# A hybrid decoder layer in which the first phase is put into program order and two query projections move between the attention's first blocks

## The chip, the cores and the metric

The kernel runs on one core of one Trainium2 chip. The metric is the device time of one execution in microseconds. Before the change it is 905.42 us (median of three runs, 904.74 to 907.59).

## The reference, cut to what matters

```python
h = rmsnorm(x, norm_mix_g)                       # 512 tokens x 1024
proj = h @ w_in                                  # one wide projection, split by columns
qk_ml, v_ml, o_ml, if_pre, q_sw, k_sw, v_sw, g_a, g_b = split(proj)
qk_ml = silu(causal_depthwise_conv(qk_ml, conv)) # 4 heads of q and k for the mLSTM
h_ml  = mlstm_chunkwise(q_ml, k_ml, v_ml, ig, lf)
y_a   = sigmoid(o_ml) * rmsnorm(h_ml)
y_b   = swa_with_sinks(q_sw, k_sw, v_sw, sinks)  # window 128, 16 query heads, 4 key heads of 64
merged = sigmoid(g_a) * (y_a @ w_branch_a) + sigmoid(g_b) * (y_b @ w_branch_b)
x = x + merged @ w_out
x = x + square(relu(rmsnorm(x) @ w_up)) @ w_down
x = x + sigmoid(rmsnorm(x) @ w_ple_gate) * (p @ w_ple_proj)
return rmsnorm(x, final_norm_g)
```

## The kernel before, in words

Tokens are handled in four tiles of 128. All large products are made from float32 operands cut into a high and a low part: ScalarE rounds the high part into `wh` (or `h`, `qs`, `yb`), VectorE subtracts it from the original and leaves the low part (`split`, lines 139 and 140). A product of two such numbers is three TensorE products, high by high, low by high, high by low (`pairs`), so one tile of 128 outputs over 1024 inputs is 24 products (`mm_T`, `mm_tok`, `chain`, line 168). A weight comes by a load from SyncE's queue into one of four `wr` buffers, and its parts go into one of four `wh` and four `wl` buffers (`load_w`).

The first phase is lines 202 to 314. A gain row is loaded into the first row of a cleared tile `grow`, and two TensorE products with a tile of ones spread it over all partitions into PSUM (`gmix`, line 251). `stir` (line 246) issues products of ones by ones that nobody reads, nine ahead of `gmix` and four behind it. `norm(m)` squares a tile of x on ScalarE (268), takes the root there (258) and the reciprocal on VectorE (260), and scales the tile in two halves (272). `turn(m)` transposes it in two groups of four blocks (285) and splits the result into `h`; `values(m)` multiplies it by 264 columns of weights in three pieces (`vsif`: attention values and mLSTM gates) and stores `vs` (297) and `gt` (299). A scheduler decides in which order each engine takes these instructions. Behind them come the two key projections (`proj_T` with `w_ksw`), the gate scans, the output gates, the mLSTM values and two gate projections.

The sliding-window attention starts with query projections 0 and 1. It then runs over 16 units of 128 queries (`units`), four heads each. `swa_probs` makes a unit's scores (636) from two query projections, reduces them on VectorE with their maximum (644), takes exponentials on ScalarE (655) and normalises (659). `swa_turn` transposes the result (670) and ScalarE copies it out (672); `swa_out` multiplies two units with the values (683). Scores and transposes take turns in two PSUM buffers, tag `a`. Units 0 to 3 use queries 0 and 1, units 4 to 7 queries 2 and 3, units 8 to 15 the other four. The remaining projections are a stock of single products, `pieces`, from which each step of the loop takes 18 to fill TensorE (708). In this stretch TensorE's order is written out by hand (`manual_schedule`); that of ScalarE and VectorE is the scheduler's.

After the loop the eighth q/k projection (`qk_proj(7)`) is made, then `silu` on all eight, the mLSTM weights (`ml_weights`, 770 to 778) and, between them, the products of branch b (`branch_b`).

Of the kernel before, what the change touches and what calls it, by code (L numbers as in the profile page):

```python
# [10 lines left out]
F32 = mybir.dt.float32  # L11
# [26 lines left out]
def block_kernel(  # L38
# [73 lines left out]
    def act_hl(n="s"):  # L112
        return [act_r(n), act_r(n)]
# [9 lines left out]
    def tok_scratch(n="lm"):  # L123
        return sp.tile([P, LMW], F32, tag="lm", bufs=LMB, name=nm(n))[:, :D]
# [5 lines left out]
    def small(n, w, bufs=4):  # L130
        return cp.tile([P, w], F32, tag=f"{n}{w}", bufs=bufs, name=nm(n))
# [4 lines left out]
    def split(dst, src, scale=None):  # L136

        if scale is None:
            done = A.copy(dst[0], src)  # L139
            V.tensor_sub(dst[1], src, r32(dst[0]))  # L140
# [48 lines left out]
    def mm_tok(ps, w, acts, m, first=True, last=True):  # L189

        ops = []
        for k in range(len(acts)):
            ops += pairs([q[:, m * P : (m + 1) * P] for q in acts[k]], [q[:, k, :] for q in w])
        chain(ps, ops, first, last)

    nc.scalar.preload_act_table_set("sqrt_and_others")


    ident = cp.tile([P, P], F32, name="ident")
    make_identity(nc, ident)  # L200
    ones = cp.tile([P, P], F32, name="ones")
    V.memset(ones, 1.0)
    eps_t = cp.tile([P, 1], F32, name="eps_t")
    V.memset(eps_t, EPS)
    zeros4 = c1.tile([4, P], F32, name="zeros4")
# [25 lines left out]
    V.memset(grow, 0.0)  # L231
    nc.sync.dma_start(out=grow[:1, :], in_=g_mix)
# [9 lines left out]
    idle = ps_a()  # L242

    def stir(n):
        for i in range(n):
            tc.keep_in_program_order(T.matmul(idle[:, :P], ones, ones, start=True, stop=True))

    stir(9)
    gmix = ps_a()
    for c in range(2):  # L250
        T.matmul(gmix[:, c * 512 : (c + 1) * 512], ones, grow[:, c * 512 : (c + 1) * 512], start=True, stop=True)
    stir(4)

    def rstd_of(ss, n):

        w = ss.shape[1]
        sd = small("sd", w)
        A.activation(sd, ss, AF.Sqrt, bias=eps_t, scale=1.0 / n)
        rs = small("rs", w, 5)
        V.reciprocal(rs, sd)  # L260
        return rs

    xns = []

    def norm(m):
        xn = tok_scratch("xn")
        ss = small("ss", 1)
        A.activation(xn, xt[m], AF.Square, accum_out=ss)
        rs = rstd_of(ss, D)
        for c in range(2):  # L270
            o = slice(c * 512, (c + 1) * 512)
            V.scalar_tensor_tensor(xn[:, o], xt[m][:, o], rs, gmix[:, o], ALU.mult, ALU.mult)
        xns.append(xn)

    vs = []
    gt = c1.tile([P, NT, 8], F32, name="gt")
    h2, hT = big_hl("h")
    hf = []

    def turn(m):  # L280
        wide = ps_a() if m == NT - 1 else None
        for kq in range(2):
            ps = wide[:, kq * 512 : (kq + 1) * 512] if wide is not None else ps_t()
            for k in range(4):
                T.transpose(ps[:, k * P : (k + 1) * P], xns[m][:, kq * 512 + k * P : kq * 512 + (k + 1) * P], ident)
            done = split(
                [t[:, 4 * kq : 4 * kq + 4, m * P : (m + 1) * P] for t in h2],
                ps.rearrange("p (k c) -> p k c", k=4),
            )
        return done  # L290

    def values(m):
        ps = ps_g()
        for (k0, n), w in zip(vsif, wv):
            mm_tok(ps[:, :264], w, hT[k0 : k0 + n], m, first=k0 == 0, last=k0 == 6)
# [25 lines left out]


    HALF = [slice(0, 64), slice(64, 128)]
    keys = []
    for i in range(2):
        ps = proj_T(w_ksw, i, ps_t)
        keys.append(act_hl("kk"))
        split(keys[i], ps)


    gml = cols(g_ml, KT, "gml", c1)
# [259 lines left out]
    def q_proj(i):  # L591
        ps = proj_T(w_qsw, i)
        q_done(i, ps)
# [11 lines left out]
    def qk_proj(i):  # L605
        qk_done(i, proj_T(w_qkml, i))
# [21 lines left out]
    def swa_probs(kp, gp, n):  # L628
        k0 = max(n - 1, 0) * P
        ls = ps_a()  # L630
        for g in range(2):
            q = qs[kp * 4 + 2 * gp + g]
            for i, (x, y) in enumerate(((0, 0), (0, 1), (1, 0))):
                for ab in range(2):
                    o = ls[:, ab * 512 + g * 256 : ab * 512 + (g + 1) * 256]
                    T.matmul(  # L636
                        o, q[x][HALF[ab], n * P : (n + 1) * P], keys[kp][y][HALF[ab], k0 : k0 + 256], start=i == 0, stop=i == 2
                    )
        W = P if n == 0 else 2 * P
        sk = sinks_of[:, kp, :, gp, :]  # L640
        lm3 = tok_scratch().rearrange("p (g k) -> p g k", g=4)[:, :, :W]
        mx = small("mx", 4)
        for g in range(4):
            V.tensor_tensor_reduce(  # L644
                lm3[:, g, :], ls[:, g * 256 : g * 256 + W], band[:, 256 - W :], 0.125, sk[:, g // 2, g % 2 : g % 2 + 1], ALU.add, ALU.max, mx[:, g : g + 1]
            )
# [12 lines left out]
        V.tensor_tensor(lm3, lm3, rc.unsqueeze(2).broadcast_to([P, 4, W]), ALU.mult)  # L659
        probs[kp, gp, n] = lm3  # L660
# [37 lines left out]

    def pieces():

        order = [("q", 3), ("k", 0), ("q", 4), ("q", 5), ("k", 4), ("q", 6), ("q", 7), ("k", 1), ("k", 5), ("k", 2), ("k", 6), ("k", 3)]
        for kind, i in order:
            w = load_w((w_qsw if kind == "q" else w_qkml)[i], KT * P, KT)
            ps = ps_g()
            for k in range(KT):
                ops = pairs([t[:, k, :] for t in w], hT[k])
                for j, (l, r) in enumerate(ops):
                    T.matmul(ps, l, r, start=k == 0 and j == 0, stop=k == KT - 1 and j == 2)  # L708
                    yield
            (q_done if kind == "q" else qk_done)(i, ps)  # L710

    fill = pieces()
    with tc.manual_schedule(engines={mybir.EngineType.PE}):
# [535 lines left out]
```

## Time and profile before

| what | value |
|---|---|
| median of three runs | 905.42 us |
| the profiled execution, whole | 905.38 us |
| its span, first to last instruction | 903.5 us |
| mean granted TensorE clock | 0.999 |
| bytes moved | 100.50 MB, mean 111 GB/s |

The profile is of one execution. Its rows name an engine, a line of the kernel, an operation and the tiles written and read; an idle time stands in brackets with the instruction that ended it. TensorE is called PE and its weight loads PEld, VectorE DVE, ScalarE ACT, GpSimd POOL, and SyncE's queue SPq. The time outside the span, 905.38 - 903.5 = 1.9 us, belongs to no instruction.

### The profile page before, as it was taken

The numbers are of one execution on the slowest core, as the hardware profiler recorded it, in microseconds if no ns is written. First come the engines' busy times: TensorE is split into PE (matmuls) and PEld (weight loads), VectorE is DVE, ScalarE is ACT, GpSimd is POOL, SyncE is SP. The second block draws the span as 40 slices with busy tenths as digits, with TensorE's granted clock in tenths as the row PEclk, the third lists the DMA queues.
The fourth block names the chain that finished last, engine by engine and source line by source line (L and its number), as shares of the span: only waits on it lengthen the run. The fifth ranks groups of instructions, "written<-read, shape, count | busy, mean of one in ns | idle before, by whom it ended". The sixth has DMA issues, their size and how long they took to land.

```text
span 903.5 us, 12111 instructions
## 1 busy us (share of the span) xinstructions
PE 886.6 (98%) x4676; PEld 741.2 (82%) x4676; DVE 645.9 (71%) x1030; ACT 451.4 (50%) x757; POOL 23.7 (3%) x40
## 2 busy tenths in 40 slices
PE   8999999999899999999999999999999999999996
PEld 7888899997677777878888888888888888888886
DVE  6884687874777787567644578757966885798466
ACT  6373444444666568675322545334434443444843
POOL 0011000000000000000310000000000000000000
PEclk9999999999999999999999999999999999999999
DMA  7543134435121133234552620631262044102302
GB/s 249 198 155 124 47 109 155 158 118 163 48 68 51 47 106 118 81 96 161 162 194 87 218 86 0 209 118 47 68 211 94 1 164 155 55 24 72 139 1 94
DMA packets 29965, 100.50 MB, mean 111 GB/s; under 512 B 4173, under 2 KB 4685, under 8 KB 29906
## 3 DMA queue, kind: packets, MB, share of 16 engines
q1 hardware_dynamic: 27938, 93.15, 30.9%
q0 software_dynamic: 1824, 6.30, 2.0%
q8 instruction: 37, 0.61, 0.3%
q10 hardware_dynamic: 144, 0.26, 0.1%
q14 instruction: 22, 0.18, 0.1%
HBM read 91.30 MB, written 8.40 MB: 110 GB/s over the span
## 4 chain that ended last, share of the span: by engine, by line
PE 72%; DVE 2%; ACT 1%; DMA 0%; issue 0%; SPq 0%; DVEq 0%; ACTq 0%
PE psg L168 35%; PE psp L168 22%; PE psg L708 7%; PE pst L168 2%; PE psa L670 2%; PE psa L636 1%; PE pst L683 1%; PE pst L777 1%; PE psp L882 1%; DVE wl L140 0%; DMA ptok<-in_p 0%; PE pst L829 0%; DVE uf L140 0%; ACT lm L655 0%; DVE lm L644 0%
## 5 line engine op out<-in xcount | busy, mean ns | idle before, releaser
L139 ACT CAST wh<-wr 128x1024 fp32r<-128x1024 f32 (+1 forms) x137 | 142.9, 1045 | 208.6 <-PE psg L168 62.8
L140 DVE TENSOR_TENSOR wl<-wr,wh 128x1024 fp32r<-128x1024 f32 (+1 forms) x137 | 171.1, 1253 | 100.4 <-ACT wh L139 91.4
L168 PE MATMUL psg<-x,wh 128*128 128x512 f32 x512 | 158.4, 390 | 0.0
L168 PE MATMUL psp<-wh,uf 128*128 128x512 f32 x448 | 139.1, 390 | 0.0
L168 PEld LDWEIGHTS psg<-x,wh 128*128 128x128 f32 x512 | 96.0, 188 | 19.9
L168 PE MATMUL psg<-x,wl 128*128 128x512 f32 x256 | 99.7, 389 | 0.0
L168 PEld LDWEIGHTS psp<-wh,uf 128*128 128x128 f32 x448 | 84.1, 188 | 17.3
L168 PE MATMUL psp<-wl,uf 128*128 128x512 f32 x224 | 87.2, 389 | 0.0
L139 ACT CAST wh<-wd 128x1024 fp32r<-128x1024 f32 x44 | 46.3, 1054 | 57.9 <-PE psp L168 26.1
L708 PE MATMUL psg<-h,wh 128*128 128x512 f32 x192 | 60.7, 397 | 0.0
L140 DVE TENSOR_TENSOR wl<-wd,wh 128x1024 fp32r<-128x1024 f32 x44 | 53.4, 1218 | 4.4 <-ACT wh L139 4.1
L168 PEld LDWEIGHTS psg<-x,wl 128*128 128x128 f32 x256 | 48.1, 188 | 9.8
L168 PE MATMUL psa<-h,wh 128*128 128x256 f32 (+1 forms) x256 | 55.1, 311 | 0.0
L168 PEld LDWEIGHTS psp<-wl,uf 128*128 128x128 f32 x224 | 42.1, 188 | 8.7
L140 DVE TENSOR_TENSOR uf<-F,uf 128x1792 fp32r<-128x1792 f32 (+2 forms) x20 | 33.0, 1650 | 21.8 <-ACT uf L139 21.8
L168 PEld LDWEIGHTS psa<-h,wh 128*128 128x128 f32 x256 | 41.9, 191 | 3.5 <-ACT p L557 0.7
L168 PE MATMUL psg<-yb,wh 128*128 128x512 f32 x128 | 42.7, 406 | 0.3 <-DVE gb L817 0.2
L139 ACT CAST uf<-F 128x1792 fp32r<-128x1792 f32 (+2 forms) x20 | 27.9, 1397 | 26.4 <-DVE F L958 26.2
L168 PE MATMUL psg<-ya,wh 128*128 128x512 f32 x128 | 40.6, 395 | 0.0
L944 DVE SCALAR_TENSOR_TENSOR rt<-psg,rB 128x512 f32<-128x512 f32 x32 | 22.0, 688 | 25.6 <-PE psg L168 25.6
L708 PEld LDWEIGHTS psg<-h,wh 128*128 128x128 f32 x192 | 34.9, 188 | 6.6
L168 PE MATMUL psg<-h,wh 128*128 128x512 f32 x128 | 40.2, 394 | 0.0
(284 smaller groups left out, 1742.0 us busy)
## 6 DMA issues: line engine op xcount, KB each, us to landing
wr<-in_w_up SPq DMA_DIRECT2D x32, 512.0 KB, 3.4
wd<-in_w_down SPq DMA_DIRECT2D x24, 512.0 KB, 4.5
wr<-in_w_o SPq DMA_DIRECT2D x8, 512.0 KB, 4.3
gd<-gr POOLq DMA_DIRECT2D x8, 512.0 KB, 3.0
wr<-in_w_qsw SPq DMA_DIRECT2D x8, 512.0 KB, 4.2
wr<-in_w_qkml SPq DMA_DIRECT2D x8, 512.0 KB, 3.2
wr<-in_w_b SPq DMA_DIRECT2D x8, 512.0 KB, 3.3
gl<-gd SPq DMA_DIRECT2D x8, 512.0 KB, 3.2
```

What stands on the lines that cost most here:

```text
L139: done = A.copy(dst[0], src)
L140: V.tensor_sub(dst[1], src, r32(dst[0]))
L168: last_mm[0] = T.matmul(ps, l, r, start=first and i == 0, stop=last and i == len(ops) - 1, skip_group_check=parts)
L636: T.matmul(o, q[x][HALF[ab], n * P : (n + 1) * P], keys[kp][y][HALF[ab], k0 : k0 + 256], start=i == 0, stop=i == 2)
L670: T.transpose(pt[:, c : c + P], lm3[:, g, j * P : (j + 1) * P], ident)
L683: T.matmul(o[HALF[ab], m * 256 : (m + 1) * 256], vs[n + m + 1 - nk + j][:, c : c + 64], pTs[m][:, j * 512 + ab * 256 : j * 512 + (ab + 1) ...
L708: T.matmul(ps, l, r, start=k == 0 and j == 0, stop=k == KT - 1 and j == 2)
L777: T.matmul(psc[:, n0:], qk[4 + h][:, n0 : n0 + P], qk[h][:, n0:], start=True, stop=True)
L882: T.transpose(ps[:, m * P : (m + 1) * P], xk[m][:, k * P : (k + 1) * P], ident)
L944: V.scalar_tensor_tensor(a, ps, 0.0, rB, ALU.max, ALU.mult)
```

## The change

The change has two parts that don't touch each other.

In the first phase, PE, ACT and DVE now take their instructions in the order in which the code is written (`manual_schedule` over all three). `ones` and half of `grow` are cleared by GpSimd, the load of the gain row stands right behind the first tile of x, and the two halves of `gmix` have a PSUM tile each. The work of `norm`, `turn` and `values` is cut into smaller helpers, and the products of the first tile follow the order in which their operands are made: the high parts with the first weights, then the low weights, then the low activations. The same products are made as before.

In the attention, queries 2 and 3 are projected whole ahead of unit 0's and unit 1's scores, 16 products of the stock follow, and each step of the loop takes 17. The eighth q/k projection joins the stock, which is 12 projections, 288 products, as before: 16 + 16 x 17.

```diff
+    ones = cp.tile([P, P], F32, name="ones")
+    G.memset(ones, 1.0)
+    grow = tok_scratch("grow")
+    G.memset(grow[:, :512], 0.0)
+    V.memset(grow[:, 512:], 0.0)
     ident = cp.tile([P, P], F32, name="ident")
     make_identity(nc, ident)
-    ones = cp.tile([P, P], F32, name="ones")
-    V.memset(ones, 1.0)
...
-    grow = tok_scratch("grow")
-    V.memset(grow, 0.0)
+    load_x(0, 2)
     nc.sync.dma_start(out=grow[:1, :], in_=g_mix)
-    load_x(0, 2)
...
-    gmix = ps_a()
+    gmix = [ps_a()[:, :512] for _ in range(2)]
     for c in range(2):
-        T.matmul(gmix[:, c * 512 : (c + 1) * 512], ones, grow[:, c * 512 : (c + 1) * 512], start=True, stop=True)
+        T.matmul(gmix[c], ones, grow[:, c * 512 : (c + 1) * 512], start=True, stop=True)
     stir(4)
...
-    norm(0)
-    turn(0)
-    wv = [load_w(None, n * 264, n, raw) for (_, n), raw in zip(vsif, wv)]
-    norm(1)
-    values(0)
-    norm(2)
-    turned = turn(1)
-    with tc.issue_after(turned):
-        norm(3)
-    values(1)
-    turn(2)
-    turn(3)
-    values(2)
-    gate_in = values(3)
+    early, late, every = range(4), range(4, 8), range(8)
+    plain = [("hi", early), ("lo w", early), ("lo h", early), ("hi", late), ("lo w", late), ("lo h", late)]
+    with tc.manual_schedule(engines={mybir.EngineType.PE, mybir.EngineType.Activation, mybir.EngineType.DVE}):
+        norm(0)
+        w_high(0)
+        scaled(0)
+        w_low(0)
+        t_ = [turn(0, kq) for kq in range(2)]
+        high(0, 0, t_[0])
+        low(0, 0, t_[0])
+        w_high(1)
+        high(0, 1, t_[1])
+        w_low(1)
+        low(0, 1, t_[1])
+        w_high(2)
+        w_low(2)
+        norm(1)
+        scaled(1)
+        ps0 = products(0, [("hi", early), ("lo w", range(3)), ("lo h", early), ("hi", late), ("lo w", range(3, 8)), ("lo h", late)])
+        t_ = [turn(1, kq) for kq in range(2)]
+        norm(2)
...
+        scaled(2)
+        ps1 = products(1, plain)
+        norm(3)
+        values(0, ps0)
+        scaled(3)
...
+        values(1, ps1)
+        ps2 = products(2, plain)
+        ps3 = products(3, plain)
+        values(2, ps2)
+        gate_in = values(3, ps3)
...
-        order = [("q", 3), ("k", 0), ("q", 4), ("q", 5), ("k", 4), ("q", 6), ("q", 7), ("k", 1), ("k", 5), ("k", 2), ("k", 6), ("k", 3)]
+        order = [("k", 0), ("q", 4), ("q", 5), ("k", 4), ("q", 6), ("q", 7), ("k", 1), ("k", 5), ("k", 2), ("k", 6), ("k", 3), ("k", 7)]
...
     with tc.manual_schedule(engines={mybir.EngineType.PE}):
+        q_proj(2)
         swa_probs(*units[0])
-        q_proj(2)
+        q_proj(3)
         swa_probs(*units[1])
+        more(16)
         for u in range(16):
             if u + LOOK < 16:
                 swa_probs(*units[u + LOOK])
             pT = swa_turn(*units[u])
-            for _ in range(18):
-                next(fill)
+            more(17)
...
-    qk_proj(7)
```

The new helpers split the old ones: `high` and `low` are the two lines of `split` for one group of four blocks, `w_high` and `w_low` those for a piece of the 264 columns, `products` issues a tile's 24 products in a given order, and `more(n)` takes n products from the stock.

How this moves instructions is seen at three places. The first is ACT at the start. In the rows, `xn` is the scaled tile, `ss` its sum of squares, `sd` the root, `wh` a weight's high part and `h` the transposed tile's. Before:

```order
L268 ACTIVATE xn_141,ss_142<-xt_101 128x1024 [waits DMAHW1_49,DMAHW0_49]
L258 ACTIVATE sd_144<-ss_142,eps_t 128x1 [waits DVE_49,Activation_49]
L139 CAST wh_164<-wr_110 128x792 [waits DMAHW2_49]
L139 CAST wh_168<-wr_112 128x792 [waits DMAHW4_49]
L139 CAST wh_172<-wr_114 128x528 [waits DMAHW5_49]
L139 CAST h_139<-pst_150 128x4x128 [waits PE_49]
L268 ACTIVATE xn_176,ss_177<-xt_102 128x1024 [waits DMAHW6_49]
L139 CAST h_139<-pst_157 128x4x128 [waits PE_49]
```

and after the change:

```order
L273 ACTIVATE xn_143,ss_155<-xt_104 128x1024 [waits DMAHW1_49,DMAHW0_49]
L275 ACTIVATE sd_157<-ss_155,eps_t 128x1 [waits DVE_49,Activation_49]
L305 CAST wh_147<-wr_111 128x792 [waits DMAHW3_49]
L295 CAST h_141<-pst_165 128x4x128 [waits PE_49]
L305 CAST wh_148<-wr_113 128x792 [waits DMAHW4_49]
L295 CAST h_141<-pst_170 128x4x128 [waits PE_49]
L305 CAST wh_149<-wr_115 128x528 [waits DMAHW5_49]
L273 ACTIVATE xn_144,ss_183<-xt_105 128x1024 [waits DMAHW6_49]
```

The second and third weight piece have moved behind the first tile's transposed halves, and the square of the second tile behind both.

The second place is DVE at the start: `rs` is the reciprocal root, `psa` the spread gain in PSUM, `wl` a weight's low part, and `h` now the transposed tile's low part. Before:

```order
L260 RECIPROCAL rs_146<-sd_144 128x1 [waits Activation_49]
L140 TENSOR_TENSOR wl_165<-wr_110,wh_164 128x792 [waits DMAHW2_49,Activation_49]
L272 SCALAR_TENSOR_TENSOR xn_141<-xt_101,rs_146,psa_131 128x512 [waits DMAHW0_49,DVE_49,PE_49]
L272 SCALAR_TENSOR_TENSOR xn_141<-xt_101,rs_146,psa_131 128x512 [waits DMAHW1_49]
L140 TENSOR_TENSOR wl_169<-wr_112,wh_168 128x792 [waits DMAHW4_49,Activation_49]
L140 TENSOR_TENSOR h_140<-pst_150,h_139 128x4x128 [waits Activation_49]
```

and after the change:

```order
L277 RECIPROCAL rs_159<-sd_157 128x1 [waits Activation_49]
L282 SCALAR_TENSOR_TENSOR xn_143<-xt_104,rs_159,psa_132 128x512 [waits DMAHW0_49,DVE_49,PE_49]
L282 SCALAR_TENSOR_TENSOR xn_143<-xt_104,rs_159,psa_133 128x512 [waits DMAHW1_49,PE_49]
L308 TENSOR_TENSOR wl_150<-wr_111,wh_147 128x792 [waits DMAHW3_49,Activation_49]
L299 TENSOR_TENSOR h_142<-pst_165,h_141 128x4x128 [waits Activation_49]
L308 TENSOR_TENSOR wl_151<-wr_113,wh_148 128x792 [waits DMAHW4_49,Activation_49]
```

Both scaled halves have moved ahead of the first weight, and each now waits for PE by itself, since each reads a PSUM tile of its own.

The third place is PE where the attention starts: the first row of each run of products, with `psg` the bank of a query projection (later of the stock), `psa` a unit's scores from keys `kk` and queries `qs`, or a transposed unit from `lm`; the products left out between them are the rest of each run. Before:

```order
L168 MATMUL psg_2079<-h_139,wh_2082 128x512
L636 MATMUL psa_2116<-kk_387,qs_2075 128x256 x2
L168 MATMUL psg_2150<-h_139,wh_2153 128x512
L636 MATMUL psa_2185<-kk_387,qs_2075 128x256 x2
L636 MATMUL psa_2219<-kk_387,qs_2075 128x256 x2
L670 MATMUL psa_2253<-ident,lm_2129 128x128 x4
```

and after the change:

```order
L168 MATMUL psg_2122<-h_141,wh_2125 128x512
L697 MATMUL psa_2157<-kk_393,qs_2081 128x256 x2
L168 MATMUL psg_2191<-h_141,wh_2194 128x512
L697 MATMUL psa_2226<-kk_393,qs_2081 128x256 x2
L769 MATMUL psg_2266<-h_141,wh_2262 128x512
L697 MATMUL psa_2283<-kk_393,qs_2081 128x256 x2
L731 MATMUL psa_2317<-ident,lm_2170 128x128 x4
```

Query 2 (psg_2150 before, psg_2122 now) stands ahead of unit 0's scores, query 3 ahead of unit 1's, and the first 16 products of the stock (psg_2266) between unit 1's and unit 2's.

More of the change, by code (lines that the diff above doesn't have):

```diff
@@ L240, in block_kernel @@
     nc.sync.dma_start(out=bif, in_=b_if.broadcast_to([P, 8]))
-    idle = ps_a()
+    idle = ps_g()
     def stir(n):
@@ L261, in rstd_of @@
         return rs
[L263 to L273, printed above, removed]
     vs = []
@@ L278, in block_kernel @@
     hf = []
[L280 to L290, printed above, removed]
@@ L292, in values, with norm @@
-    def values(m):
-        ps = ps_g()
-        for (k0, n), w in zip(vsif, wv):
-            mm_tok(ps[:, :264], w, hT[k0 : k0 + n], m, first=k0 == 0, last=k0 == 6)
+    xns = [tok_scratch("xn") for _ in range(NT)]
+    rss = {}
+    def norm(m):
+        ss = small("ss", 1)
+        A.activation(xns[m], xt[m], AF.Square, accum_out=ss)
+        sd = small("sd", 1)
+        A.activation(sd, ss, AF.Sqrt, bias=eps_t, scale=1.0 / D)
+        rss[m] = small("rs", 1, 5)
+        V.reciprocal(rss[m], sd)
@@ new lines, in scaled, with turn, parts @@
+    def scaled(m):
+        for c in range(2):
+            o = slice(c * 512, (c + 1) * 512)
+            V.scalar_tensor_tensor(xns[m][:, o], xt[m][:, o], rss[m], gmix[c], ALU.mult, ALU.mult)
+    def turn(m, kq):
+        ps = ps_t()
+        for k in range(4):
+            T.transpose(ps[:, k * P : (k + 1) * P], xns[m][:, kq * 512 + k * P : kq * 512 + (k + 1) * P], ident)
+        return ps
+    def parts(m, kq):
+        o = slice(4 * kq, 4 * kq + 4)
+        return [t[:, o, m * P : (m + 1) * P] for t in h2]
@@ new lines, in high, with low, w_high @@
+    def high(m, kq, ps):
+        return A.copy(parts(m, kq)[0], ps.rearrange("p (k c) -> p k c", k=4)).ins
+    def low(m, kq, ps):
+        hi, lo = parts(m, kq)
+        return V.tensor_sub(lo, ps.rearrange("p (k c) -> p k c", k=4), r32(hi)).ins
+    wvh = [wp.tile([P, 1024], F32R, tag="wh", bufs=WB, name=nm("wh"))[:, : n * 264] for _, n in vsif]
+    wvl = [wp.tile([P, 1024], F32R, tag="wl", bufs=WB, name=nm("wl"))[:, : n * 264] for _, n in vsif]
+    def w_high(i):
+        A.copy(wvh[i], wv[i][:, : vsif[i][1] * 264])
@@ new lines, in w_low, with products @@
+    def w_low(i):
+        V.tensor_sub(wvl[i], wv[i][:, : vsif[i][1] * 264], r32(wvh[i]))
+    def products(m, order):
+        ps = ps_g()
+        where = {k0 + k: (i, k) for i, (k0, n) in enumerate(vsif) for k in range(n)}
+        done = 0
+        for kind, ks in order:
+            for k in ks:
+                i, c = where[k]
+                act = hT[k][1 if kind == "lo h" else 0][:, m * P : (m + 1) * P]
+                w = (wvl if kind == "lo w" else wvh)[i][:, c * 264 : (c + 1) * 264]
+                last_mm[0] = T.matmul(ps[:, :264], act, w, start=done == 0, stop=done == 3 * KT - 1)
+                done += 1
+        return ps
@@ L296, in values @@
+    def values(m, ps):
         t = sp.tile([P, 256], F32, tag="vs", bufs=4, name=nm("vs"))
@@ L299, in values @@
         return V.tensor_add(gt[:, m, :], ps[:, 256:264], bif)
-    norm(0)
-    turn(0)
-    wv = [load_w(None, n * 264, n, raw) for (_, n), raw in zip(vsif, wv)]
-    norm(1)
-    values(0)
-    norm(2)
-    turned = turn(1)
-    with tc.issue_after(turned):
-        norm(3)
-    values(1)
-    turn(2)
-    turn(3)
-    values(2)
-    gate_in = values(3)
+    early, late, every = range(4), range(4, 8), range(8)
[19 more added lines that the diff above has]
+        norm(2)
+        high(1, 0, t_[0])
+        high(1, 1, t_[1])
+        low(1, 0, t_[0])
+        low(1, 1, t_[1])
+        scaled(2)
+        ps1 = products(1, plain)
+        norm(3)
+        values(0, ps0)
+        scaled(3)
+        t_ = [turn(2, kq) for kq in range(2)]
+        q = [ps_a()[:, :512] for _ in range(2)]
+        for kq in range(2):
+            high(2, kq, t_[kq])
+            low(2, kq, t_[kq])
+        for kq in range(2):
+            for k in range(4):
+                T.transpose(q[kq][:, k * P : (k + 1) * P], xns[3][:, kq * 512 + k * P : kq * 512 + (k + 1) * P], ident)
+        for kq in range(2):
+            turned = [high(3, kq, q[kq]), low(3, kq, q[kq])]
+        values(1, ps1)
[3 more added lines that the diff above has]
+        gate_in = values(3, ps3)
+    turned.append(last_mm[0].ins)
     def proj_T(wd, i, bank=ps_g):
@@ L323, in block_kernel @@
     HALF = [slice(0, 64), slice(64, 128)]
[L324 to L328, printed above, removed]
+    with tc.issue_after(turned[0]), tc.issue_after(turned[1]), tc.issue_after(turned[2]):
+        keys = []
+        for i in range(2):
+            ps = proj_T(w_ksw, i, ps_t)
+            keys.append(act_hl("kk"))
+            split(keys[i], ps)
     gml = cols(g_ml, KT, "gml", c1)
@@ L712, in block_kernel, with more @@
     fill = pieces()
+    def more(n):
+        for _ in range(n):
+            next(fill)
     with tc.manual_schedule(engines={mybir.EngineType.PE}):
+        q_proj(2)
         swa_probs(*units[0])
-        q_proj(2)
+        q_proj(3)
         swa_probs(*units[1])
+        more(16)
         for u in range(16):
```

## The prediction

> **What bounds the kernel now.** I read the page first, then the table of stretches, then TensorE's waits, then the timeline of the places where TensorE waits.
>
> ```profile
> PE 886.6 (98%) x4676; PEld 741.2 (82%) x4676; DVE 645.9 (71%) x1030; ACT 451.4 (50%) x757; POOL 23.7 (3%) x40
> ```
>
> TensorE (PE) is busy for 98% of the span, so the other engines matter only where PE waits for them. The next view shows where that is. A row gives start:end, its length, then the busy time of PE, of its weight loads (PEld), of VectorE (DVE), ScalarE (ACT) and GpSimd.
>
> ```profile
> 0.00:32.00 32.00, 28.79 (x172) 24.56 (x173) 19.92 (x36) 18.53 (x32) 2.05 (x11) 1.00 0.75 264
> 30.50:200.00 169.50, 169.49 (x1048) 151.44 (x1047) 128.14 (x158) 78.61 (x96) 8.54 (x19) 1.00 0.36 124
> 220.00:230.70 10.70, 7.79 (x55) 6.37 (x53) 6.46 (x28) 3.33 (x12) 0.00 (x0) 1.00 0.28 100
> 230.70:243.60 12.90, 12.56 (x80) 9.55 (x78) 9.84 (x30) 9.64 (x32) 0.00 (x0) 1.00 0.13 41
> 243.60:336.20 92.60, 92.59 (x587) 71.80 (x587) 71.34 (x211) 60.34 (x165) 0.00 (x0) 1.00 0.18 58
> 336.20:362.00 25.80, 25.29 (x109) 19.55 (x108) 21.13 (x37) 20.31 (x44) 0.00 (x0) 1.00 0.41 142
> ```
>
> From 30.5 to 200 us PE is never idle, and in most of the attention (243.6 to 336.2) neither. What can be won lies in the first 30 us and around 216 to 244 us. PE's waits there, in total, times, longest:
>
> ```profile
> PE psa L670 <- DVE mx L644: 2.9, 1, 2.9
> PE psa L636 <- DVE qs L140: 1.2, 2, 0.9
> PE psa L636 <- ACT qs L139: 0.9, 1, 0.9
> PE pst L777 <- DVE dm L778: 0.5, 1, 0.5
> ```
>
> The first three are 5.0 us, all at the attention's start.
>
> **The change, term A: until the first tile is turned.** These are rows of the timeline: start, length, engine, line, operation, and in brackets the idle time before.
>
> ```profile
> 1.06 4.21 PE L246 MATMUL psa<-ones 128*128 128x128 f32 x18 [1.06 <-DVE eps_t L204]
> 1.30 0.91 DVE L231 MEMSET grow<- 128x1024 f32 x1 [0.16 <-issue]
> 1.66 0.42 SPq L149 DMA_DIRECT2D wr<-in_w_vsif  x1
> 2.24 0.30 SPq L232 DMA_DIRECT2D grow<-in_g_mix  x1
> 5.99 3.75 PE L251 MATMUL psa<-grow,ones 128*128 128x512 f32 x4 [0.73 <-DMA grow<-in_g_mix]
> 6.03 0.16 DVE L260 RECIPROCAL rs<-sd 128x1 f32<-128x1 f32 x1 [3.82 <-ACT sd L258]
> 9.54 1.26 PE L246 MATMUL psa<-ones 128*128 128x128 f32 x8
> 9.78 1.41 DVE L272 SCALAR_TENSOR_TENSOR xn<-xt,rs,psa 128x512 f32<-128x512 f32 x2 [1.50 <-PE psa L251]
> 10.68 1.22 PE L285 MATMUL pst<-ident,xn 128*128 128x128 f32 x8
> 28.83 0.62 PE L168 MATMUL pst<-h,wh 128*128 128x512 f32 x2
> ```
>
> The gain row is loaded at 2.24, because DVE clears 1024 columns of its tile until 2.21; a weight load has gone ahead of it at 1.66. PE idles 0.73 us for it. After the change GpSimd and DVE clear 512 columns each, and the load stands ahead of the weights. Half of 0.91 us puts its issue at 1.66, so it lands some 0.6 us earlier or more; PE then goes on at 5.27, where its first row ends: **0.7 us**.
>
> Next come the two broadcasts of the gain, four records in 3.75 us, and four filling matmuls, eight records in 1.26 us. Eighteen records of the same filling matmuls took 4.21 us before 5.27, so PE ran at half its rate until about 9.54. When it doubles in the changed kernel the trace can't show. It can be no earlier than 5.27, since 4.21 us of unbroken work didn't bring it; as recorded it came 3.55 us after the gap. Between those ends I take the middle, 7.4. Then the broadcasts are issued at 5.27 and 6.98, the second speeds up after a quarter, and PE is through at 8.04; the fillers take 0.85 more, and the first tile's transposes start at 8.9 instead of 10.68. DVE doesn't hold them: its first half waits for the first broadcast only (7.2), and takes 0.74. **Term A: -1.8 us.** If PE keeps the half rate until 9.54, the transposes start at 9.97 (-0.7); if it doubles at 5.27, at 7.85 (-2.8).
>
> The Trainium skill (TensorE: Matmul & The Clock Gate, Part 1: The HAM clock gate) says that the array runs at half rate until it has been busy through one window of about 3.4 us, that the windows run freely, and that the doubling thus comes 3.4 to 6.8 us after work begins. For work unbroken from 1.06 us that is 4.5 to 7.9 us. By this rule, which the row at 9.54 fits if the 0.73 us gap spoilt a window, term A would lie between -1.6 and -2.8; the rule speaks against the half rate until 9.54.
>
> **Term B: from the first transposes to the first key projection.** Before, this took 28.83 - 10.68 = 18.15 us.
>
> ```profile
> 8.60 0.63 ACT L139 CAST wh<-wr 128x528 fp32r<-128x528 f32 x1 [0.32 <-DMA wr<-in_w_vsif]
> 15.56 1.03 PE L285 MATMUL pst<-ident,xn 128*128 128x128 f32 x8
> 16.19 1.07 ACT L139 CAST h<-pst 128x512 fp32r<-128x512 f32 x2
> 17.15 1.07 ACT L268 ACTIVATE xn<-xt 128x1024 f32<-128x1024 f32 x1
> 25.83 0.40 PE L168 MATMUL psg<-wh,h 128*128 128x264 f32 x2
> 28.71 0.28 PE L168 MATMUL psg<-wh,h 128*128 128x264 f32 x1
> ```
>
> Products of one tile: from 25.83 to 28.71, 24 at 0.12 = 2.88 us. Eight transposes take about 0.9. Four tiles are 15.1 us at best, so 3.0 us were waits.
>
> The first tile gets worse. ACT now rounds weight pieces 1 and 2 behind the first tile's halves (before, both were done by 9.23), and squares tile 1 after that. From the first transposes: 0.6 until four are out, then ACT 0.5 (half of the 1.07 pair), 0.8 (a 792 wide piece, scaled from the 0.63 for 528), 0.5, 0.5, then the square 1.2, root 0.3, DVE's reciprocal and first half 0.9, hand-overs 0.2: tile 1 is turned 5.5 us after tile 0. It was 15.56 - 10.68 = 4.9: **+0.6**. From there: three tiles of 2.88 and 24 transposes are 11.3 us; I leave 0.6 for the hand-overs that remain, as DVE scales tiles 2 and 3 while PE multiplies tile 1, and tile 3's transposes stand ahead of tile 2's products. That is 11.9 against 28.83 - 15.56 = 13.3: **-1.4**. **Term B: -0.8 us**, with 0 (a second lag like tile 1's) and -3.0 (no wait left) as ends.
>
> ACT rounds the first key weights only after tile 1's values, and SyncE waits with its third output-gate load for that.
>
> ```profile
> 6.42 2.23 SPq L149 DMA_DIRECT2D wr<-in_w_ksw  x2
> wr<-in_w_ksw SPq DMA_DIRECT2D x2, 512.0 KB, 8.7
> ```
>
> The key weights are issued from 6.42 us on and land 8.7 us later, by about 17; ACT comes to them at some 22, four before PE needs them. PE's 169.49 of 169.50 us behind shows that no later load is short, so I cost both at nothing; a late weight would cost one DVE pass, 1.2 us (the row at 226.69 below).
>
> **Term C: the attention's start.**
>
> ```profile
> 216.81 0.62 PE L636 MATMUL psa<-kk,qs 64*128 64x256 f32 x6
> 220.08 5.67 PE psg L168 x24
> 225.68 1.69 PE L636 MATMUL psa<-kk,qs 64*128 64x256 f32 x24
> 226.69 1.23 DVE L140 TENSOR_TENSOR wl<-wr,wh 128x1024 fp32r<-128x1024 f32 x1 [2.17 <-PE psa L636]
> 227.83 0.68 DVE L140 TENSOR_TENSOR qs<-psg,qs 128x512 fp32r<-128x512 f32 x1
> 230.05 0.47 DVE L644 CUSTOM_DVE_ANT_0 lm<-psa,band,sink 128x256 f32<-128x256 f32 x1
> 230.27 0.63 PE L670 MATMUL psa<-ident,lm 128*128 128x128 f32 x4 [2.91 <-DVE mx L644]
> ```
>
> Unit 0's scores start at 216.81, directly behind query 1's last product, and wait 0.9 + 0.9 us for its split. The changed order puts query 2's 24 products (5.67 us in the chain's row) between: the wait goes, and nothing takes its place. Query 3's weights move one load ahead in SyncE's queue; four query loads follow one another, one per 5.67 us of products, and they land in 4.2:
>
> ```profile
> wr<-in_w_qsw SPq DMA_DIRECT2D x8, 512.0 KB, 4.2
> ```
>
> Then PE waits 2.91 us to turn unit 0, as that writes the PSUM buffer from which DVE reads unit 1's scores, and DVE came to them late, behind a weight and a query split (226.69, 227.83). Now 16 products and unit 2's scores stand between, 16 x 0.24 + 0.9 = 4.7 us. DVE needs, from unit 1's last score, at most a query split (0.68) and four reductions (4 x 0.47): 2.6 us, in time even with a weight (1.23) ahead. What is left of the waits for queries, 1.2 - 0.9 = 0.3 us for query 3's split at unit 4, goes too: query 3 is complete three steps earlier. That is -5.0. For one more switch between kinds of products I add 0.15: unit 0's first score starts 0.1 us later behind a projection product than another product would. **Term C: -4.85 us.** Ends: -5.0, and -2.1 if the 2.91 us return.
>
> Seventeen products per step instead of 18 leave DVE 0.24 us less per step. It is busy 71.34 of 92.60 us, so I cost that at nothing.
>
> **Term D: the end.** Projection 7, 5.4 us of PE work, stood behind the attention as cover and now stands inside.
>
> ```profile
> 334.30 1.95 PE L683 MATMUL pst<-pT,vs 128*64 128x256 f32 x16
> 336.25 11.33 PE psg L168 x49
> 349.91 1.28 ACT L770 ACT_TABLE_LOAD   x1
> ```
>
> Its 24 of those 49 products end at about 341.8; ACT then rounds, convolves and takes eight sigmoids until 349.91. After the change the last output matmuls (1.95 us) stand behind these products, so PE starts branch b 2.0 us later against ACT than before. ACT's last rounding ahead of the exponentials must wait until branch b's first 24 products (5.4) free a weight buffer, with two weight matmuls among them some 8.7 us behind projection 7; before, ACT was there after 7.1 (349.91, less one pass of 1.0). So ACT's chain slips by 1.7, PE's by 2.0; they cancel, and the 0.5 us wait stays. **Term D: 0**, at worst +1.7.
>
> **Sum.** -1.8 - 0.8 - 4.85 = -7.45 us against the profiled execution's own 905.38 us (span 903.5 and 1.9 around it), which is within 0.04 of the median 905.42: **897.9 us**. From branch b on PE's order is the same row for row.
>
> **Rivals.** *The half rate stays until 9.54:* term A is -0.7, 899.0 us. For it: the only doubling recorded. Against: work is unbroken from 1.06 now. *The first phase gains nothing:* ACT's and DVE's fixed order costs what A brings; 905.38 - 4.85 = 900.5. For it: tile 1 lags already. Against: the floor of 15.1 us. *The turn of unit 0 waits again*, so the change doesn't do there what it says: 905.38 - 7.45 + 2.9 = 900.8. For it: DVE's queue is set by a scheduler. Against: 4.7 us of cover. *Slower:* DVE falls behind in the loop. If each of 16 steps waits for a score buffer, the gain is eaten at 7.45 / 16 = 0.47 us per step; with 0.7 the time is 905.38 - 7.45 + 11.2 = 909.1. For it: DVE is 77% busy and the steps shorten. Against: 0.01 us of PE idle in 92.6 us now.
>
> **How the numbers follow.** Forecast 0.52, half rate 0.20, nothing in the first phase 0.12, turn waits 0.09, slower 0.03, and 0.04 for several of the losses at once, which leaves some 904. The range reaches from the best ends of A and B in part (-2.8, -1.6 and C: 896.0) to the two rivals near 901 with C's loose end: 895.8 to 901.5. Measurement can tell about 0.3%, 2.7 us, from no change; so faster means below 902.7: 0.93, same 0.04, slower 0.03.
>
> **What would show it.** PE's first broadcast at about 5.3 and transposes at 8.9; tile 1 turned 5.5 us after; the first key product at 26.2; no wait over 0.3 us of PE's score matmuls or turns; the 0.5 us wait before the weights' matmuls still there. I would be wrong if the first key product came after 28, or the loop showed PE waiting for DVE's reductions.

## The result, and the profile after

The changed kernel takes 897.28 us (median of 5 runs, 897.05 to 897.59); before beside it 906.64 us (904.74 to 909.84). The ratio is 0.9895, with a 95% interval of 0.9872 to 0.9918. The profiled execution took 897.05 us, with a span of 895.3 us; before's took 905.38 us. Forecast were 897.9 us and 895.8 to 901.5.

The page's row of busy times, then the table of stretches of the changed kernel (start:end, length, busy time of PE, PEld, DVE, ACT and GpSimd, PE's granted clock, DMA share, GB/s):

```profile
PE 884.4 (99%) x4676; PEld 739.9 (83%) x4676; DVE 644.8 (72%) x1029; ACT 450.1 (50%) x757; POOL 24.3 (3%) x42
```

```profile
0.00:28.00 28.00, 26.22 (x171) 23.47 (x172) 18.88 (x34) 18.36 (x32) 2.67 (x13) 1.00 0.78 274
212.00:235.00 23.00, 23.00 (x127) 18.26 (x125) 13.45 (x43) 12.16 (x30) 0.00 (x0) 1.00 0.24 79
235.00:330.00 95.00, 94.65 (x612) 73.30 (x611) 75.57 (x229) 63.25 (x182) 0.00 (x0) 1.00 0.17 54
```

PE did the same work (4676 instructions, 2.2 us less busy), and its idle time went. At the attention's start, where it idled 5 us, it is now busy for 23.00 of 23.00 us. The rows of PE's timeline at the places that the prediction named:

```profile
1.00 4.21 PE L247 MATMUL psg<-ones 128*128 128x128 f32 x18 [1.00 <-POOL ones L200]
5.00 1.97 PE L252 MATMUL psa<-grow,ones 128*128 128x512 f32 x4
7.70 1.04 PE L287 MATMUL pst<-ident,xn 128*128 128x128 f32 x8
13.19 1.29 PE L287 MATMUL pst<-ident,xn 128*128 128x128 f32 x8 [0.23 <-ACT xn L273]
25.06 0.62 PE L168 MATMUL pst<-h,wh 128*128 128x512 f32 x2
218.51 0.97 PE L697 MATMUL psa<-kk,qs 64*128 64x256 f32 x12
230.81 0.66 PE L731 MATMUL psa<-ident,lm 128*128 128x128 f32 x4
324.74 0.71 PE L769 MATMUL psg<-h,wh 128*128 128x512 f32 x2 [0.35 <-DVE acc L673]
451.74 0.47 PE L168 MATMUL psp<-wh,mg 128*128 128x512 f32 x1 [0.88 <-ACT wh L139]
```

The broadcasts no longer wait, and their four records take 1.97 us instead of 3.75: the array is at its full rate from about 5.0 us on. The first tile is turned at 7.70 (forecast 8.9), the second 5.49 us later (forecast 5.5), the first key product starts at 25.06 (forecast 26.2, before 28.83). Unit 0's scores and its turn (218.51, 230.81) have no brackets, so nothing is waited for there. The last two rows are new waits. The second matters below: 0.88 us in front of the first product into the psp tile (the PSUM tile of the product with `w_out`), 118 us behind branch b's start.

Four landmarks of PE cut each execution into pieces: the first key product, branch b's first product (psg<-yb), the first psp product, and the span's end. I worked the pieces out as differences of starts in each kernel's timeline. All kernels of the experiments are in this table, and the text refers to it.

| kernel | to first key product | on to branch b | on to psp | on to the end |
|---|---|---|---|---|
| before | 28.83 | 312.92 | 117.51 | 444.24 |
| changed | 25.06 | 308.12 | 118.56 | 443.56 |
| changed, again | 25.49 | 308.11 | 118.55 | 443.65 |
| changed, a third time | 24.66 | 308.38 | 118.61 | 443.65 |
| first phase alone | 24.93 | 314.24 | 118.69 | 443.54 |
| attention alone | 26.82 | 308.07 | 117.47 | 443.84 |
| attention alone, again | 27.69 | 308.55 | 117.55 | 443.91 |
| gain row early | 27.98 | 316.28 | 117.70 | 443.54 |
| 12 filling matmuls | 27.42 | 313.55 | 117.56 | 443.87 |
| no cover | 26.04 | 308.54 | 118.56 | 443.56 |
| cover only | 27.23 | 313.24 | 117.58 | 444.05 |
| waits filled | 27.18 | 312.69 | 118.03 | 443.80 |
| other bank | 25.13 | 308.62 | 117.50 | 443.45 |
| other bank, weight first | 25.37 | 308.35 | 117.49 | 443.59 |

From before to changed the columns give -3.77, -4.80, +1.05 and -0.68: -8.2 us, the difference of the spans.

### The profile page after: what moved, and what is told of

The parts are those of the page before. It is cut to its first block, busy times and chain, and to the rows that moved or that the text cites. A ratio compares the mean times of both kernels' runs of the same rounds, so it can differ in the third digit from the quotient of the medians.

```text
span 895.3 us, 12110 instructions
## 1 busy us (share of the span) xinstructions
PE 884.4 (99%) x4676; PEld 739.9 (83%) x4676; DVE 644.8 (72%) x1029; ACT 450.1 (50%) x757; POOL 24.3 (3%) x42
## 4 chain that ended last, share of the span: by engine, by line
PE 92%; DVE 4%; ACT 3%; issue 0%; POOL 0%; DVEq 0%; POOLq 0%
PE psg L168 45%; PE psp L168 23%; PE psa L168 10%; PE psg L769 4%; PE pst L168 3%; ACT lm L716 1%; PE psa L697 1%; PE psg L319 1%; PE psa L731 1%; DVE acc L673 1%; PE pst L842 1%; PE pst L744 1%; DVE lm L705 1%; PE psp L947 1%; DVE lm L720 1%; PE psg L247 1%
## 5 line engine op out<-in xcount | busy, mean ns | idle before, releaser
L139 ACT CAST wh<-wr 128x1024 fp32r<-128x1024 f32 x134 | 140.6, 1052 | 211.6 <-PE psg L168 61.7
L140 DVE TENSOR_TENSOR wl<-wr,wh 128x1024 fp32r<-128x1024 f32 x134 | 168.5, 1262 | 97.1 <-ACT wh L139 90.1
L769 PE MATMUL psg<-h,wh 128*128 128x512 f32 x192 | 61.6, 397 | 0.4 <-DVE acc L673 0.4
L716 ACT ACTIVATE lm<-lm,nmx 128x256 f32<-128x256 f32 (+1 forms) x64 | 30.0, 470 | 23.6 <-DVE nmx L709 23.6
L139 ACT CAST uf<-F 128x1792 fp32r<-128x1792 f32 (+2 forms) x20 | 27.9, 1397 | 26.3 <-DVE F L1023 26.2
```

## The experiments

My theory was that the first phase is worth 3.8 us, about half of it (3.75 - 1.97 = 1.8 us in the broadcasts) an earlier doubling of the array's rate that unbroken work brings; that the attention is worth the length of its waits; and that the two add up. The rivals stand in the expectations.

### The two parts, each alone

The first kernel has the changed first phase and before's attention; the second the reverse. Their diffs are the two halves of the change's diff.

> The changed first phase with the attention and its end as before. If the two parts add up: the first key product at 25.06 us as in the changed kernel (28.83 before), the attention's waits of 0.9, 0.9, 0.3 and 2.9 us back, and the time 3.8 us below before's, about 901.6 us (ratio 0.9958). Rival (the first phase's gain is swallowed later, by a load or by DVE): within 1 us of before, or a new wait of about 2 to 4 us between 30 and 215 us.

> The first phase as before, the attention's start, its loop and projection 7 as changed. If the parts add up: first key product at 28.8 us, PE waits for nothing over 0.4 us between 215 and 365 us, and the time 4.4 to 4.85 us below before's, 900.5 to 901.0 us (ratio 0.995). Rival (the attention gains only because the first phase ends earlier, or the other way round, the 0.9 us wait at a psp product of the changed kernel is the price of its new end): under 4.0 us gained.

Measured: the first phase alone 903.79 us (902.92 to 908.09, 10 runs), the attention alone 898.48 (897.97 to 898.53), before beside them 904.88 (903.08 to 908.13). The ratios are 0.9998 (0.998 to 1.0016) and 0.9933 (0.9918 to 0.9948). So the first phase shows no gain that can be told from none, and the attention gains 6.4 us, more than the waits that it lost. Neither was expected.

The first phase's rival holds in part. Its trace reaches the first key product 3.9 us before the profiled execution of before, and then waits anew. PE's waits between 30 and 210 us, and the one at psp:

```profile
PE psa L168 <- ACT p L618: 0.8, 1, 0.8
PE psa L168 <- DVE t L612: 0.3, 1, 0.3
```

```profile
457.86 0.47 PE L168 MATMUL psp<-wh,mg 128*128 128x512 f32 x1 [0.88 <-ACT wh L139]
```

The rest of the difference between the profiled executions is at the start of the attention's trace: its first phase is before's, line for line, and yet it doesn't wait for the gain row, and reaches the first key product at 26.82 us, 2.0 us earlier than the profiled before.

```profile
5.07 2.23 PE L251 MATMUL psa<-grow,ones 128*128 128x512 f32 x4
```

So what I had read in before's trace as the first phase's cost was in part the chance of one execution. The next runs ask how much.

### What the first phase is worth when the attention doesn't disturb

> Before's first phase with the changed attention again, beside the changed kernel: what the first phase is worth by itself, with nothing of the old attention in the way. If it is worth what the profiled executions showed (first key product 28.83 against 25.06 us): 3.8 us more than the changed kernel, less the 0.9 us of the psp wait which only the new first phase has, so 900.2. If the profiled execution of before was a late one: first key product at 26.8 us again, 1.75 us later than in the changed kernel, less 0.9, so about 0.9 us more than it: 898.2.

> The changed kernel again, as the yardstick for the runs beside it. Broadcasts start where the first row of filling matmuls ends, without idle time; they take between 1.9 us (array doubled before them) and 3.6 us (not doubled), as the doubling falls anew in each execution: first key product between 25.0 and 26.7 us. No PE wait over 0.5 us between 200 and 365 us; the 0.9 us wait of a psp product near 452 us again. Time 897.0 to 897.6 us, clock 0.998 to 0.999 in each run.

Measured beside each other: the attention alone 899.32 us (898.26 to 900.32), the changed kernel 897.68 (897.08 to 898.55). The difference is 1.6 us, between the two cases. Here the gain row came later still, and the array was at its full rate when it came:

```profile
6.61 1.96 PE L251 MATMUL psa<-grow,ones 128*128 128x512 f32 x4 [1.34 <-DMA grow<-in_g_mix]
```

Before's first phase was recorded five times (before, attention alone twice, cover only, waits filled). Its wait for the gain row was 0.73, 0, 1.34, 0.34 and 0.32 us, and its first key product came at 28.83, 26.82, 27.69, 27.23 and 27.18, 27.55 on average. The changed first phase was also recorded five times, never with a wait for the row: 24.66 to 26.04, 25.24 on average. The gain is thus some 2.3 us, of which about 1.05 is given back at psp in each of the five (118.55 to 118.69; 117.51 in before).

### One edit each: the row, the unbroken work

```diff
+    ones = cp.tile([P, P], F32, name="ones")
+    G.memset(ones, 1.0)
+    grow = tok_scratch("grow")
+    G.memset(grow[:, :512], 0.0)
+    V.memset(grow[:, 512:], 0.0)
...
-    grow = tok_scratch("grow")
-    V.memset(grow, 0.0)
-    nc.sync.dma_start(out=grow[:1, :], in_=g_mix)
     load_x(0, 2)
+    nc.sync.dma_start(out=grow[:1, :], in_=g_mix)
```

> Before with one edit alone: the clearing of the gain row's tile is split between GpSimd and VectorE, and the row's load goes ahead of the weights. If the idle 0.73 us in front of the broadcasts is what kept the array at half rate: broadcasts at about 5.0 us without idle time, four records in about 2.0 us instead of 3.75, first transposes at about 7.8 us (10.68 before), that is nearly the whole of the changed kernel's 2.98 us up to there. Rival (the array doubles at a time after the start, or because of the other order of the instructions): broadcasts at 5.3 us but still over 3 us long, transposes at about 9.9. The first key product follows by the same amount in both if ACT and DVE hold nothing back: at about 26 or 28.1 us.

```diff
-    stir(9)
+    stir(12)
```

> Before with one edit alone: 12 filling matmuls ahead of the broadcasts instead of 9; the gain row comes as late as before. If unbroken work is enough: no idle time ahead of the broadcasts, which start at about 6.0 us as before but run 2.0 us instead of 3.75, and the first transposes stand at about 9.0 us instead of 10.68. Rival (the rate depends on when the row lands, or on the time since the start): broadcasts still 3.75 us long, transposes at 10.6 us or later.

Measured (one execution each): 907.36 and 904.27 us. The broadcasts of the two:

```profile
5.00 2.99 PE L252 MATMUL psa<-grow,ones 128*128 128x512 f32 x4
```

```profile
1.05 5.49 PE L246 MATMUL psa<-ones 128*128 128x128 f32 x24 [1.05 <-DVE eps_t L204]
6.34 1.98 PE L251 MATMUL psa<-grow,ones 128*128 128x512 f32 x4
```

Both stood between the two answers, and the runs above say why: the doubling falls differently in each execution. A broadcast record takes 0.89 us at half rate (3.55 / 4, before) and 0.45 at the full one (1.80 / 4, changed), so the four of the early row held the half rate for 2.3 records, until about 7.1 us; with 12 filling matmuls it ended at about 6.3, in the changed kernel at 5.0, and in the first phase alone at 4.3, as there the 18 filling records took 3.63 us instead of 4.00. Against 26.82 to 28.83 for before's first phase, 27.98 and 27.42 show no gain. An early row alone isn't enough: the first transposes stood at 8.92 us, and then ScalarE's and VectorE's parts of the first tile came late by 0.53 and 0.69 us. The gain of 2.3 us needs the written order of those engines too. How much of it each edit brings I can't tell from single executions that scatter by 1 to 2 us.

The first of these traces holds something else. In the 2.9 us wait of unit 0's turn, which it shares with before, PE's granted clock falls, 2 us after the wait began, and stays low behind it:

```profile
227.00:229.00 2.00, 0.03 (x2) 0.00 (x0) 2.00 (x7) 0.00 (x0) 0.00 (x0) 1.00 0.20 41
229.50:235.50 6.00, 5.56 (x15) 4.55 (x16) 4.70 (x20) 4.70 (x19) 0.00 (x0) 0.50 0.12 46
236.00:240.00 4.00, 4.00 (x31) 3.19 (x30) 1.76 (x8) 0.54 (x1) 0.00 (x0) 1.00 0.01 2
```

The third figure from the end is the clock: 0.50 for six us. Three 128x512 products of the stock took 1.28 us there (232.10 to 233.38 in the timeline), and 0.68 at the same place in before's (232.11 to 232.79). From unit 0's first scores to branch b pass 127.78 us here (216.48 to 344.26), 2.8 more than in before's trace (216.81 to 341.75), where the clock stayed at 1.00.

### The cover: taken away, and put into before

The cover is the 16 products between unit 1's scores and the loop.

```diff
         swa_probs(*units[1])
-        more(16)
...
-            more(17)
+            more(18)
```

> The changed kernel without the 16 products between unit 1's scores and the loop, 18 products per step again. If they are the cover: PE waits some 2 to 3 us for VectorE's reductions ahead of unit 0's turn. If such a wait costs its own length alone: about 900 us in each run, with the clock at 0.998 to 0.999 as without it. If the wait also lets the array fall back to half rate in some executions (as the profile of the kernel with the early gain row shows at 229.5 to 235.6 us, behind the same wait): a median of 901 or more, a spread of some 3 us and clocks down to 0.995 or less. Rival (VectorE is early here because of query 2's new place): no wait over 0.5 us, 897.5 us.

The second kernel does the same to before the other way round: 16 products behind unit 1's scores, then 17 per step.

> Before with 16 of the loop's products moved ahead of unit 0's turn and 17 per step, nothing else: the waits of 0.9 and 0.9 us for query 1 stay, the 2.9 us wait goes. If a wait costs its own length: 2.3 to 2.9 us less than before, and a spread and clocks like before's (0.991 to 0.999). If the 2.9 us wait is also what lets the array's rate fall: all clocks at 0.997 or more, a spread under 1 us, and a median 4 us or more below before's.

Measured: without the cover 898.12 us (897.26 to 898.45) beside the changed kernel's 897.68; the cover alone 903.81 (901.82 to 905.97) beside before's 906.3, ratio 0.9977 (0.9956 to 0.9997). The wait comes back, but half as long:

```profile
226.09 1.69 PE L697 MATMUL psa<-kk,qs 64*128 64x256 f32 x24
229.27 0.63 PE L731 MATMUL psa<-ident,lm 128*128 128x128 f32 x4 [1.49 <-DVE mx L705]
```

Both theories were half right. In before, VectorE came to unit 1's reductions behind a weight (1.23 us) and a query split; with the queries in their new places only the split is ahead. So of 2.9 us the queries' order takes about half, the cover the other half, and the stretch to branch b grows by only 0.2 to 0.4 us without it: products that aren't cover here stand in for others in the loop, and the 0.35 us wait at 324.74 goes. No clock fell behind the shorter wait (0.998 to 0.999 in all five runs).

In before, the cover takes the 2.9 us wait away, and gets a wait of 1.25 us for a convolution in the loop in its place. But the clocks still fall, behind the two waits for query 1's split that this kernel keeps:

```profile
216.77 0.50 PE L636 MATMUL psa<-kk,qs 64*128 64x256 f32 x4 [0.89 <-ACT qs L139]
218.14 0.39 PE L636 MATMUL psa<-kk,qs 64*128 64x256 f32 x2 [0.87 <-DVE qs L140]
```

```profile
215.00:219.00 4.00, 2.23 (x16) 1.38 (x15) 2.15 (x5) 2.81 (x3) 0.00 (x0) 1.00 0.10 23
219.50:222.50 3.00, 3.00 (x8) 2.32 (x8) 1.15 (x9) 1.74 (x9) 0.00 (x0) 0.50 0.21 82
223.00:227.00 4.00, 4.00 (x27) 3.05 (x26) 0.25 (x1) 1.33 (x2) 0.00 (x0) 1.00 0.01 4
```

PE was idle for 0.9 us at a time, not longer, and busy for 2.23 of 4 us. Then its products ran at half rate: eight records of query 2 in 3 us, where at 0.68 us for three, as before's timeline has them, some 13 would fit. The expectation that the 2.9 us wait alone lets the rate fall is wrong. The median is 2.5 us below before's, as expected for a wait that costs its own length.

### The waits filled with work

This kernel leaves before's order and puts matmuls of ones into the three waits.

```diff
+                if fill_in and g == 1 and i != 1:
+                    stir(4, fill_in)
...
-        swa_probs(*units[0])
+        swa_probs(*units[0], fill_in=ps_t())
...
+            if u == 0:
+                stir(12, ps_t())
             pT = swa_turn(*units[u])
```

> Before with the waits at the attention's start filled with matmuls of ones whose results nobody reads: 4 and 4 inside unit 0's scores, 12 ahead of unit 0's turn. Unit 0's scores and turn start when they started before, or up to 0.5 us later, so the waits' own length stays as a cost. If those waits cost their own length only: time and spread as before's (median within 1 us, 903 to 910, clocks 0.992 to 0.999). If they also let the array fall back to half rate: no clock under 0.997, a spread under 2 us, and a median 2 to 4 us below before's, near its fastest runs (903).

Measured: 903.72 us (902.92 to 905.98, 11 runs) beside before's 905.12 (902.75 to 908.45, 15 runs); ratio 0.9987 (0.9974 to 0.9999). The waits are full, and last as long as they did (from first scores to turn 13.7 us; in before 216.81 to 230.27, 13.5):

```profile
215.24 0.62 PE L638 MATMUL psa<-kk,qs 64*128 64x256 f32 x6
215.78 1.16 PE L246 MATMUL pst<-ones 128*128 128x128 f32 x8
217.30 1.16 PE L246 MATMUL pst<-ones 128*128 128x128 f32 x8
225.99 2.94 PE L246 MATMUL pst<-ones 128*128 128x128 f32 x24
228.97 0.63 PE L672 MATMUL psa<-ident,lm 128*128 128x128 f32 x4
```

So nothing was gained but the rate: 10 of 11 runs have a mean clock of 0.997 or more, and the median is 1.4 us lower. It was less than the 2 to 4 us that I expected (the spread, 3.1 us instead of under 2, missed too), and in the direction of that theory. The same reading of before's own 45 runs beside the experiments: 17 with a clock of 0.997 or more have a median of 903.97 us, 23 with 0.995 or less one of 906.37. Where in those runs the clock was low their means don't tell; of the five traces that keep two or all three of the waits unfilled (before, the first phase alone, the early row, 12 filling matmuls, the cover only), the early row's and the cover's have the fall at the attention's start, and the other three have none.

### The wait that came 450 us later

The change has an edit that its diff above leaves out: the tile into which the filling matmuls write, taken from pool `a` before (`idle = ps_a()`), now comes from psg (`idle = ps_g()`). The first of the next kernels takes it from pst.

```diff
-    idle = ps_g()
+    idle = ps_t()
```

> The changed kernel beside its two variants: 897.0 to 898.6 us in each run, the 0.9 us wait of the first psp product at about 452 us.

> The changed kernel with one edit: the filling matmuls at the start write a PSUM buffer of the pool pst instead of psg. In the order of the kernel's instructions the first psp product then waits for ScalarE alone, as in before, and no longer for VectorE too. If the changed kernel's 0.9 us wait near 452 us comes from there (the psp tile takes over banks of the psg pool, whose turn has moved on by one buffer, so it waits for VectorE's reading of the gate product at 450.90 us): the wait is gone, from branch b's first product to the first psp product pass 117.5 us instead of 118.56, and the time is 0.9 to 1.0 us less, about 896.5. Rival (the wait is for ScalarE's weight, as the waits' table names it): it stays, time as beside.

> As the kernel beside it, and ScalarE rounds the second weight piece before the first tile's first half instead of between its halves. If the piece has landed by about 7.7 us, ScalarE is through with tile 0 some 0.6 us earlier and tile 1 is turned 4.9 us after tile 0 instead of 5.5: another 0.4 to 0.6 us, about 896.0. Rival (the piece lands later): PE waits up to 1 us more ahead of the first value products, same or 0.5 us slower.

Measured: changed kernel 897.33 us (897.03 to 898.02), other bank 896.43 (896.12 to 896.65), with the weight first as well 896.40 (895.81 to 896.92); ratios to before 0.9912, 0.9900 (0.9887 to 0.9914) and 0.9900. The wait at psp is gone, and with it 1.1 us of the table's third column. The first psp product with the other bank (PE), and VectorE's reading of the gate product:

```profile
451.25 0.39 PE L168 MATMUL psp<-wh,mg 128*128 128x512 f32 x1
```

```profile
451.45 0.69 DVE L920 TENSOR_TENSOR sga<-psg,gl 128x512 f32<-128x512 f32 x1 [1.64 <-PE psg L168]
```

In the changed kernel the same reading ran until 451.59, and psp's first product followed at 451.74. The rows of its timeline, ScalarE's weight pass, VectorE's reading and the load of the product's own weights:

```profile
450.68 1.04 ACT L139 CAST wh<-wr 128x1024 fp32r<-128x1024 f32 x1 [2.44 <-PE psg L168]
450.90 0.69 DVE L920 TENSOR_TENSOR sga<-psg,gl 128x512 f32<-128x512 f32 x1 [1.63 <-PE psg L168]
451.71 0.19 PEld L168 LDWEIGHTS psp<-wh,mg 128*128 128x128 f32 x1 [1.27 <-ACT wh L139]
```

With the other bank the product starts before that reading; it no longer waits for VectorE. The waits' table names ScalarE, whose weight pass ended at nearly the same time (451.72), and was misleading here: the product's weights were being loaded at 451.71, before that pass had ended, and with the other bank the product starts at 451.25, when the same pass (451.23 to 452.28) has hardly begun. That the tile's banks follow the turn of the psg pool I infer from the edit; the trace doesn't show banks.

The weight's earlier place does locally what was expected (the second row is cut off by its view, with six of eight records):

```profile
5.00 2.72 PE L252 MATMUL psa<-grow,ones 128*128 128x512 f32 x4
8.44 0.82 PE L287 MATMUL pst<-ident,xn 128*128 128x128 f32 x6
13.50 1.29 PE L287 MATMUL pst<-ident,xn 128*128 128x128 f32 x8
```

Tile 1 is turned 5.06 us after tile 0, not 5.49. But in this execution the array doubled late (broadcasts 2.72 us), and the time is the same as without it. Both kernels beat before and the changed kernel; which of them is better the runs don't tell.

## Why the prediction was right, and where not

- **Term C, the attention's start (-4.85):** right. The stretch from the first key product to branch b is 4.80 us shorter in the profiled pair, and 4.4 to 4.9 in the four other traces of the changed attention without another edit. Before's trace, from which I took it, has the shortest such stretch of the five kernels that keep old waits (312.92 to 316.28). The term's ground was half right: I gave the whole 2.9 us wait to the cover, and the queries' order does half of it.
- **Term A, the first tile (-1.8):** mis-sized. It measured -2.98 in the profiled pair, beyond my end of -2.8: 1.0 from the start of the broadcasts (I had 0.7), the rest from the rate. I had let the array double at 7.4 us, the middle of two ends; it had doubled by 5.0. The lower end was no bound: that 4.21 us of unbroken work had brought no doubling by 5.27 was true of one execution, and with the first phase alone it came at 4.3. (My 1.71 us for a broadcast at half rate and 0.85 for the fillers are small slips: the rows give 3.55 / 2 = 1.78, and 0.90 from 6.80 to 7.70. And before's row at 9.54, 1.26 us for eight records that take 1.05 in the others, shows that its doubling came some 0.4 us later than I read.) The larger error was of kind: I took 28.83 and the 0.73 us gap for the kernel's, and they were one execution's, the latest of five.
- **Term B, to the first key product (-0.8):** right, -0.79, with the second tile's lag of 5.49 us (5.5 in the sum) and 11.87 from there to the first key product (11.9).
- **Term D and the rest (0):** the wait ahead of the weights' matmul stayed (0.38 us, 0.51 before). "From branch b on PE's order is the same row for row" was true of the order, and not enough: a wait of 0.9 us came there, from a PSUM buffer taken 450 us earlier. With 0.7 us won elsewhere behind it, it cost little.
- **The rivals:** the half rate did not stay until 9.54 us, and no step of the loop waits for a score buffer (one wait of 0.35 us in 95). "Nothing in the first phase" came nearest, though not by its ground, the fixed order: alone, in before's company, the first phase gained nothing that could be told from none.
- **What no term held:** idle time at the attention's start lets the array fall to half its rate in some executions, for 3.4 and 6.8 us in the two traces that show it; by the mean clocks it is about half of before's runs (23 of 45 at 0.995 or less). The change ends that, worth some 1.4 us in the median by the filled waits. The profiled execution of before had the late start and had no such fall, so its 905.38 us stood at the median by two chances of opposite sign. That my sum came out is luck in part, for that reason too: the first phase is worth about 1.3 us (2.3 less 1.05; 1.6 in the medians beside each other), not 2.6, and the attention 6.4 to 7.0, not 4.85.

The Trainium skill (TensorE: Matmul & The Clock Gate, Part 1: The HAM clock gate) says that the array's doubling varies from run to run because its window runs freely. The traces agree: with unbroken work from 1.0 us on it came between about 4.3 and 7.1 us. By this rule there was no reason to take before's 9.54 us for the kernel's own. The 3.4 to 6.8 us that the prediction gives with this page is an estimate of mine from its window.

## What to carry to other kernels

A wait of TensorE costs its length and, in some executions, the half rate behind it; look at the granted clock around each wait, over several runs, before pricing it. What one trace shows in its first 10 us may be that execution's alone: record the same lines twice before building a term on them. And a scratch tile taken from a rotating pool moves the turn of every later buffer of it, so that a wait can arise half a kernel later.

## What the runs showed of the hardware

The fall to half rate needed no long idle time. With the turn's wait, 2.9 us idle, the clock was 0.50 for some 6.8 us (229.1 to 235.9); with two waits of 0.9 us it was 0.50 for some 3.4 us (219.3 to 222.7). The Trainium skill (TensorE: Matmul & The Clock Gate, Part 1: The HAM clock gate) puts the fall behind an idle window of about 3.4 us; here PE had been busy for 2.23 of the 4 us before it, and the measurement decides.

The trace files keep a list of the times at which the clock changed. With the early row it rose at 7.21 us, fell at 229.08 and rose at 235.91; with the cover only it rose at 4.25, fell at 219.29 and rose at 222.70. The low stretches last 3.41 us and twice that (6.83), and the falls come 221.87 and 215.04 us behind the first rise, 65 and 63 times 3.413. So in these two traces the clock changed at points some 3.41 us apart, which lie differently in each execution. That may be one reason why the same waits cost the rate in one execution and not in another, but it isn't shown. In the 3.41 us ahead of the falls PE was busy for 1.36 and 1.66 us; in before, one such stretch (228.41 to 231.82, counted from its rise at 9.96) held 1.55 us of work, and the clock stayed up. PE's busy time alone doesn't decide, and what does stays open.

At the program's start the profile's clock column can't be used: it reads 1.00 from 0 to 28 us in the changed kernel, while its filling matmuls take 0.22 us each up to 5.0 us (18 in 4.00) and 0.11 behind (8 in 0.90). There the rate shows in the records' lengths, and in the list of changes, which begins with a rise at 5.17.
